# Two products of a decoder block, from packed float32 parts to scaled float16 parts

## The chip, the cores and the metric

One core of a Trainium2 chip runs the whole block as one program. The metric is the device time of one execution in microseconds (us); three timed executions are given, and one further execution was recorded by the profiler. Engines are named as the profile does: PE is TensorE (PEld its weight loads), DVE is VectorE, ACT is ScalarE, POOL is GpSimd, and SP is SyncE, which issues most transfers.

## The reference, cut to what matters

The block normalises its input, multiplies it by one wide matrix, runs dilated attention and a causal convolution side by side, merges the two under sigmoid gates, mixes the result, and ends with a SwiGLU layer. All is float32 with 1024 tokens and 1024 channels. The part around the change is:

```python
o = einsum('gbsh,gbshd->bshd', alpha, stack(outs))        # attention output, 1024 x 512
y_attn = o @ w_attn_out                                   # 512 x 1024: the attention output's product
y_conv = silu(layer_norm(conv(u))) @ w_conv_out + b_conv_out
merged = sigmoid(z_ga) * y_attn + sigmoid(z_gc) * y_conv
x = x + rms_norm(merged @ w_mix_out, g_post_mix)          # 1024 x 1024: the mixing product
h = rms_norm(x, g_pre_ffn)
x = x + rms_norm((silu(gate) * up) @ w_ffn_out, g_post_ffn)   # gate, up from h @ w_ffn_in
```

## The kernel before, in words

Every product is made of two-part operands: a value is split into a rounded first part (hi) and the remainder (lo), and a product is hi by hi, hi by lo and lo by hi, three matmuls. Most products have float16 parts, scaled by powers of two from sums of squares so that nothing leaves float16's range: `two` gives one buffer for both parts, `scaled_parts` writes hi on ACT (L330) and lo on DVE (L331). The attention output's product (jobs `ao`), the mixing product (jobs `mx`) and the last product of the block have packed float32 parts without a scale instead: hi by a copy on ACT (L320), lo by a subtraction (L321) on DVE for a weight tile's first half and on the engine `wsplit` for its second, which is POOL in these two products.

The order of the work on each engine is that of the Python program. `tick` is called after every three matmuls; it advances generators that stand in the background (`bg`), such as `early_scales`, `merge` and `mix_norm`, each of which yields the number of ticks until its next step. So the program's text sets where in each engine's queue a step stands, and the times set only who waits.

The stages, with start and end in us of the profiled span:

- 206 to 331, gate pairs (`gate_pair`): two-by-two products by Winograd's scheme (`winograd`, matmuls at L501 to L503), whose bank X is filled, copied by ACT (L515, L520, L525) and filled again, while DVE runs the convolution (L885) and POOL prepares sums.
- 331 to 540, query and key pairs, in the same scheme. `early_scales` runs behind them: it loads 20 weight tiles of 128x1024 (12 of the value weights, 8 of the convolution's output weights) one after another, ACT squares and sums each (L208), and at the end of a group DVE makes the scale.
- 540 to 853, value products, attention (exponentials L1251, transposes L1274, evictions L1279), and the convolution's output product (L485 to L489, as all products by `unit`). For each of four pairs of heads `merge` adds the three dilations' outputs into O[0], a tile of 128x1024, PE transposes it (L1363) and ACT evicts it (L1366). The first two go to DRAM and come back through `out_parts`, the last two are split at once.
- 853 to 897, the attention output's product: eight column blocks n, two halves of 512 tokens each, 12 matmuls per half. DVE multiplies each half by the attention's gate (L1753) and adds the convolution's half under its gate (L1754); ACT makes hi of the sum (L1756), DVE lo (L1759), one half later. There are six PSUM banks of the kind that products use.
- 897 to 990, the mixing product (L1794): row tiles 0 and 1 together, while the weight tiles arrive, then six tiles one by one, 48 matmuls each. After each tile `mix_norm` runs in the background: `residual` (Square on ACT at L1492, `rstd_rows` at L1479 to L1484, DVE at L1499 and L1503), then Square and scaling of the new row (L1514, L1516), and after four tiles transposes (L1524) with eviction on ACT (L1530).
- 990 to 1617, the SwiGLU layer, which the diff doesn't touch.

`total` and `bound` turn partial sums of the 128 partitions into one power of two: PE multiplies a column by a matrix of ones (L146), DVE halves the exponent (L147, L149).

The lines have other numbers in the changed kernel. Those of which the text speaks: L208 becomes L230; L320, L321 and L330, L331 become L381 and L382; L515, L520, L525 become L566, L571, L576; L1251 becomes L1302; L1279 becomes L1330; L1366 becomes L1424; L1753, L1754, L1756, L1759 become L1814, L1815, L1817, L1820; L1492 becomes L1552. The Square in `merge` is L1406.

Of the kernel before, what the change touches and what calls it, by code (L numbers as in the profile page):

```python
# [9 lines left out]
F32 = mybir.dt.float32  # L10
# [8 lines left out]
T = 1024  # L19
# [52 lines left out]
class Build:  # L72
# [77 lines left out]

    def scales(self, i):
# [15 lines left out]
    def input_scales(self):  # L167
# [4 lines left out]
        for c in (C_PRE, C_PREF):  # L172
            m = self.tiny(2, "pk", 4)
            nc.scalar.activation(self.junk[:, :8], self.col8(c), AF.Square, scale=1 / H_TOP, accum_out=m[:, 0:1])
            p.append(self.total(m, 1))
        yield 6
        for e, c in enumerate((C_PRE, C_PREF)):
# [3 lines left out]
            self.bound(t[:, 0:1], p[e])  # L181
# [9 lines left out]
    def early_scales(self, groups):  # L191

        nc = self.nc
        m = self.small.tile([128, 24], F32, name="em")
        t = self.small.tile([128, 5], F32, name="cs")
        self.conv_bias = self.small.tile([128, 8], F32, name="cb")
        for c, x, k in ((0, C_GLN, 32), (1, C_BLN, 1)):
            nc.scalar.activation(self.junk[:, :8], self.col8(x), AF.Square, scale=k * A_TOP, accum_out=m[:, c:c + 1])
        pa = self.total(m[:, 0:2], 2)
        yield 6  # L200
        self.bound(t[:, 0:1], pa)
        nc.vector.reciprocal(t[:, 1:2], t[:, 0:1])
        yield 2
        todo = [(e, j) for e, jobs in enumerate(groups) for j in jobs]
        x, ends = None, {len(jobs) + 2 + sum(len(y) for y in groups[:e]): e for e, jobs in enumerate(groups)}
        for n in range(2, len(todo) + 3):
            if x is not None:
                nc.scalar.activation(self.junk, x, AF.Square, scale=W_TOP, accum_out=m[:, n - 1:n])  # L208
            x = None
            if n < len(todo) + 2:  # L210
                x = self.slot()
                nc.sync.dma_start(x, self.jobs[todo[n - 2][1]][0])
            yield 3
            if n in ends:
# [10 lines left out]
                for j in jobs:  # L225
                    self.scale[j] = tuple(u[:, i:i + 1] for i in range(1, 5))
            else:
                yield 8
        w = self.scale[groups[1][0]][0]
        nc.vector.tensor_tensor(t[:, 4:5], t[:, 0:1], u[:, 0:1], op=OP.mult)  # L230
        nc.vector.tensor_scalar(self.conv_bias, self.col8(C_BCO), t[:, 1:2], w, op0=OP.mult, op1=OP.mult)
        nc.vector.tensor_scalar(self.vun, self.scale[groups[0][0]][1], 1 / (KEEP * P_TOP), None, op0=OP.mult)
        self.act_scale, self.conv_un = t[:, 1:2], t[:, 4:5]
# [1085 lines left out]
    def merge(self, hp, st, last):  # L1319
# [34 lines left out]
        yield 2 + 2 * late  # L1354
        if hp < 2:
            hi = self.slot()
        else:
            hi, lo = self.slot(F32R), self.slot(F32R)
# [826 lines left out]
```

## Time and profile before

| | us |
|---|---|
| median of three timed executions | 1623.63 (1623.48 to 1623.65) |
| the profiled execution, its own time | 1622.73 |
| its span, first to last instruction | 1621.0 |
| PE, DVE, ACT, POOL busy | 1594.3, 1244.2, 997.3, 448.8 |
| mean granted clock of TensorE | 0.998 |

The profiled execution lies 0.9 us below the median, and its span 1.7 us below its own time. Busy time of PE is that of pipelined matmuls whose recorded durations overlap: how fast they follow one another is read from start to start. In a row of a timeline a bracket gives the idle time of the engine ahead of the instruction and who ended it; in the chain a row has start, duration, engine and line, and a count where rows were joined.

### The profile page before, as it was taken

What the parts mean: (1) busy time and instruction counts of PE and PEld (TensorE: products, weight loads), DVE (VectorE), ACT (ScalarE), POOL (GpSimd) and SP (SyncE); (2) the same over time, 40 slices, a digit from 0 to 9 for tenths busy, and PEclk for the clock granted to TensorE, in tenths of its full rate; (3) what the DMA queues carried; (4) which work ended last, traced back from release to release, by engine and by line L of the source; (5) the groups of instructions that cost most, each with busy time, mean ns of one, the idle gap of its engine ahead of it and who ended that gap; (6) DMA issues with size and microseconds to landing.
All of it is one profiled execution on the core that took longest, in us unless ns stands there. A gap on an engine that the chain in (4) does not pass through costs nothing.

```text
span 1621.0 us, 25348 instructions
## 1 busy us (share of the span) xinstructions
PE 1594.3 (98%) x9034; PEld 980.5 (60%) x9034; DVE 1244.2 (77%) x2415; ACT 997.3 (62%) x1900; POOL 448.8 (28%) x372
## 2 busy tenths in 40 slices
PE   8999999999999999999999999999999999999998
PEld 6744444444444799976658786444444444588886
DVE  6879999988898768797777655876666666667686
ACT  6476666777776578877743576645455555444453
POOL 0006777767777343654401200000000000000000
PEclk9999999999999999999999999999999999999999
DMA  4352333455665666768847422043222331684334
GB/s 175 109 208 104 111 136 144 151 188 188 202 181 144 215 189 171 179 209 242 256 153 269 180 95 91 27 146 127 104 98 98 130 124 72 233 305 118 136 105 156
DMA packets 158906, 254.02 MB, mean 157 GB/s; under 512 B 63313, under 2 KB 82444, under 8 KB 158780
## 3 DMA queue, kind: packets, MB, share of 16 engines
q1 hardware_dynamic: 154572, 240.23, 44.5%
q0 software_dynamic: 3920, 11.91, 2.3%
q8 instruction: 71, 1.16, 0.3%
q14 instruction: 55, 0.45, 0.1%
q10 hardware_dynamic: 288, 0.27, 0.0%
HBM read 178.52 MB, written 78.55 MB: 159 GB/s over the span
## 4 chain that ended last, share of the span: by engine, by line
PE 83%; DVE 8%; ACT 3%; POOL 2%; issue 2%; DMA 1%; SPq 0%; DVEq 0%; POOLq 0%; ACTq 0%
PE p L2069 13%; PE p L501 13%; PE p L503 13%; PE p L502 13%; PE p L1794 4%; PE p L485 4%; PE p L489 4%; PE p L487 4%; PE p L1142 2%; PE p L1144 2%; PE p L1146 2%; DVE p L885 2%; PE p L739 2%; PE p L1274 2%; PE p L1237 2%
## 5 line engine op out<-in xcount | busy, mean ns | idle before, releaser
L501 PE MATMUL p<-b,b 128*128 128x512 f16 x1032 | 390.9, 379 | 2.1 <-ACT c L515 1.6
L503 PE MATMUL p<-b,b 128*128 128x512 f16 x1032 | 391.1, 379 | 1.5 <-POOL b L340 1.5
L502 PE MATMUL p<-b,b 128*128 128x512 f16 x1032 | 391.0, 379 | 0.0
L2069 PE MATMUL p<-b,b 128*128 128x512 f32 x924 | 211.4, 391 | 1.9 <-DVE c L1977 1.9
L2069 PEld LDWEIGHTS p<-b,b 128*128 128x128 f32 x924 | 174.5, 189 | 38.8 <-DVE c L1977 2.3
L503 PEld LDWEIGHTS <-b 128*128 128x128 f16 x1032 | 100.8, 98 | 125.3 <-POOL b L340 4.0
L501 PEld LDWEIGHTS <-b 128*128 128x128 f16 x1032 | 100.9, 98 | 121.3
L502 PEld LDWEIGHTS <-b 128*128 128x128 f16 x1032 | 100.8, 98 | 119.2 <-issue 3.0
L885 DVE SCALAR_TENSOR_TENSOR p<-b,par,p 128x511 f32<-128x511 f32 (+14 forms) x232 | 164.5, 742 | 0.0
L485 PE MATMUL p<-b,b 128*128 128x512 f16 (+1 forms) x368 | 141.3, 384 | 1.6 <-ACT b L330 1.6
L489 PE MATMUL p<-b,b 128*128 128x512 f16 (+1 forms) x368 | 140.7, 382 | 0.4 <-DVE b L331 0.4
L487 PE MATMUL p<-b,b 128*128 128x512 f16 (+1 forms) x368 | 140.6, 382 | 0.0
L331 DVE SCALAR_TENSOR_TENSOR b<-d,sc,b 128x1024 f16<-128x1024 f32 x40 | 51.2, 1281 | 87.7 <-ACT b L330 87.7
L340 POOL TENSOR_TENSOR b<-d,b 128x1024 f16<-128x1024 f32 x44 | 93.9, 2133 | 83.8 <-ACT b L339 83.8
L1146 PE MATMUL p<-b,b 128*128 128x256 f16 x384 | 104.7, 273 | 0.0
L1142 PE MATMUL p<-b,b 128*128 128x256 f16 x384 | 104.7, 273 | 0.0
L1144 PE MATMUL p<-b,b 128*128 128x256 f16 x384 | 104.7, 273 | 0.0
L1399 ACT CAST b<-b 128x512 fp32r<-128x512 f32 (+1 forms) x117 | 72.1, 617 | 43.4 <-PE p L2069 20.4
L1400 DVE TENSOR_TENSOR b<-b,b 128x512 fp32r<-128x512 f32 (+1 forms) x117 | 80.1, 688 | 19.6 <-ACT b L1399 18.2
L1794 PE MATMUL p<-b,b 128*128 128x512 f32 x384 | 90.2, 392 | 0.0
L1251 ACT ACTIVATE c<-c,stat 128x128 f32<-128x128 f32 (+1 forms) x192 | 84.3, 443 | 6.8 <-DVE stat L1241 6.7
L515 ACT COPY c<-p 128x512 f32<-128x512 f32 x43 | 25.2, 585 | 99.6 <-PE p L503 64.1
(296 smaller groups left out, 3431.9 us busy)
## 6 DMA issues: line engine op xcount, KB each, us to landing
b<-w_in SPq DMA_DIRECT2D x30, 512.0 KB, 5.7
b<-w_v SPq DMA_DIRECT2D x24, 512.0 KB, 4.6
b<-w_fi SPq DMA_DIRECT2D x24, 512.0 KB, 4.4
d<-w_in SPq DMA_DIRECT2D x23, 512.0 KB, 3.6
dqS<-c SPq DMA_DIRECT2D x44, 256.0 KB, 2.0
b<-w_fo SPq DMA_DIRECT2D x44, 256.0 KB, 4.9
c<-dqS SPq DMA_DIRECT2D x44, 256.0 KB, 4.4
d<-w_fi SPq DMA_DIRECT2D x20, 512.0 KB, 3.7
```

The source lines that it names most:

```text
L485: nc.tensor.matmul(ps, hi[:, s], a, start=kt == 0, stop=False)
L487: nc.tensor.matmul(ps, hi[:, s], b, start=False, stop=False)
L489: nc.tensor.matmul(ps, lo[:, s], a, start=False, stop=kt == nk - 1)
L501: nc.tensor.matmul(ps, hi[:, s], a, start=first and kt == 0, stop=False, skip_group_check=True)
L502: nc.tensor.matmul(ps, hi[:, s], b, start=False, stop=False, skip_group_check=True)
L503: nc.tensor.matmul(ps, lo[:, s], a, start=False, stop=kt == 3, skip_group_check=True)
L885: nc.vector.scalar_tensor_tensor(A[i][:, j:], src[i][:, :H - j], w[i], A[i][:, j:], op0=OP.mult, op1=OP.add)
L1142: nc.tensor.matmul(o, a, hi[:, s], start=kt == 0, stop=False)
L1144: nc.tensor.matmul(o, a, lo[:, s], start=False, stop=False)
L1146: nc.tensor.matmul(o, b, hi[:, s], start=False, stop=kt == KT - 1)
L1794: nc.tensor.matmul(banks[tt][nh], st, wt[:, nh * H:(nh + 1) * H], start=bool(kt == 0 and a), stop=bool(kt == KT - 1 and b))
L2069: nc.tensor.matmul(acc[t], x, y, start=first and e == 0, stop=last and e == 2, skip_group_check=True)
```

## The change

Both products take two float16 parts under powers of two. Their matmuls keep their number and shapes, 192 and 384.

- The jobs `ao` and `mx` join the set of float16 jobs, so their weights are split by `scaled_parts`, ACT and DVE, each half; POOL has no part in it any more (15 subtractions fewer). Each product's operands lie in one buffer where there were two.
- `early_scales` has four groups (12, 8, 8, 8 tiles), 36 loads and Squares for 20, starts with the gate pairs and has one tile every 12 ticks for 13. It also makes constant factors for what follows.
- In each `merge` ACT squares O[0] with a running sum ahead of the transposes' evictions; the evictions apply a scale. After the last merge `mix_scales` (one transpose on PE, nine operations on DVE) makes the mixing product's scale from the four sums.
- In the attention output's product L1753 and L1759 become operations with a scale, L1756 a scaled copy.
- `residual` has one more DVE multiply of 128x1 (rr by the factor that takes the scale out), and its Square's scale comes from a tile.
- `root` and `largest` take the place of `total` and `bound` in `input_scales` and `early_scales`: a 128x128 transpose on PE and a maximum on DVE for the matmul with ones.

```diff
     def early_scales(self, groups):
...
-        for n in range(2, len(todo) + 3):
+        for n in range(len(todo) + 1):
             if x is not None:
-                nc.scalar.activation(self.junk, x, AF.Square, scale=W_TOP, accum_out=m[:, n - 1:n])
+                k = self.jobs[todo[n - 1][1]][1]
+                nc.scalar.activation(self.junk[:, :k], x[:, :k], AF.Square, scale=W_TOP, accum_out=m[:, n - 1:n])
...
-                yield 8
+                yield 7
...
+    def mix_scales(self):
+        nc = self.nc
+        r, on = self.osq[:, 4:5], self.osq[:, 5:6]
+        nc.vector.tensor_reduce(r, self.osq[:, :4], AX.X, OP.add)
+        yield 4
+        self.root(on, r)
+        y = self.mix_un
+        nc.vector.scalar_tensor_tensor(y, on, self.att_top, self.conv_top, op0=OP.mult, op1=OP.add)
+        self.power(y, y)
+        nc.vector.tensor_scalar(y, y, 2.0 ** -14, TINY, op0=OP.mult, op1=OP.max)
+        nc.vector.reciprocal(self.mix_scale, y)
+        nc.vector.tensor_tensor(y, y, self.mix_w, op=OP.mult)
+        nc.vector.tensor_scalar(self.mix_root, y, ROOT, None, op0=OP.mult)
...
         yield 2 + 2 * late
+        nc.scalar.activation(self.junk, O[0], AF.Square, scale=self.o_scale, accum_out=self.osq[:, hp:hp + 1])
...
-            hi, lo = self.slot(F32R), self.slot(F32R)
+            hi, lo = self.two(T)
...
-            nc.scalar.copy(a, y)
             if hp > 1:
-                nc.vector.tensor_tensor(lo.rearrange("p (m u) -> p u m", u=8)[:, h * 4:h * 4 + 4], y, f(a),
-                                        op=OP.subtract)
+                nc.scalar.activation(a, y, AF.Copy, scale=self.o_scale)
+                nc.vector.scalar_tensor_tensor(lo.rearrange("p (m u) -> p u m", u=8)[:, h * 4:h * 4 + 4], y,
+                                               self.o_scale, a, op0=OP.mult, op1=OP.subtract)
+            else:
+                nc.scalar.copy(a, y)
...
-            self.OT[hp] = self.both(x)
+            self.OT[hp] = self.both(x, self.o_scale, True)
...
         r = self.rstd_rows(ss[:, 1:2], ss[:, 2:3])
+        nc.vector.tensor_tensor(r, r, self.mix_un, op=OP.mult)
...
-    B.f16 = {*range(glu_jobs[3][0], ao[0]), *range(B.fi0, len(J))}
-    B.early = [i for p in vj.values() for i in p] + co
+    B.f16 = {*range(glu_jobs[3][0], len(J))}
+    B.early = [i for p in vj.values() for i in p] + co + ao + mx
...
+    es = B.bg(B.early_scales((B.early[:12], co, ao, mx)))
     for n in range(4):
         B.gate_pair(B.d_ga[2 * n:2 * n + 2], ga[n])
...
-            nc.vector.tensor_tensor(c[:, s], ps, c[:, s], op=OP.mult)
+            nc.vector.scalar_tensor_tensor(c[:, s], ps, B.att_un, c[:, s], op0=OP.mult, op1=OP.mult)
             nc.vector.scalar_tensor_tensor(c[:, s], y[:, s], B.conv_un, c[:, s], op0=OP.mult, op1=OP.add)
-            x = B.slot(F32R)
-            nc.scalar.copy(x[:, :H], c[:, s])
+            x = B.packed()
+            nc.scalar.activation(x[:, :H], c[:, s], AF.Copy, scale=B.mix_scale)
...
-            rest = lambda x=x, c=c[:, s]: nc.vector.tensor_tensor(x[:, H:], c, f(x[:, :H]), op=OP.subtract)
+            rest = lambda x=x, c=c[:, s]: nc.vector.scalar_tensor_tensor(x[:, H:], c, B.mix_scale, x[:, :H],
+                                                                         op0=OP.mult, op1=OP.subtract)
```

Where the instructions stand now is shown at three places; a row has line, operation, output and input with buffer numbers, and the tile's shape (x2: two such in a row).

ACT in a gate pair, before and after, from the scaling of a gate half to the second copy of bank X. The tile em collects the weights' sums.

```order
L339 CAST b_1987<-d_1953 128x1024
L978 ACTIVATE c_1843<-c_1843,sc_1693 128x512
L995 ACTIVATE c_2001<-p_1840,sc_1693 128x512
L515 COPY c_2005<-p_2003 128x512
L165 ACTIVATE d_1922<-d_1922,sc_2019 128x1024
```

```order
L390 CAST b_2016<-d_1982 128x1024
L1029 ACTIVATE c_1845<-c_1845,sc_1695 128x512
L1046 ACTIVATE c_2030<-p_1842,sc_1695 128x512
L230 ACTIVATE junk,em<-b_1974 128x1024
L566 COPY c_2034<-p_2032 128x512
L187 ACTIVATE d_1949<-d_1949,sc_2048 128x1024
```

A weight Square (L230) stands ahead of the copy of bank X; another stands ahead of the next pair's copies at other points, since 12 ticks don't divide a pair.

ACT in the first merge (hp = 0), before and after: exponentials (L1251, now L1302), evictions of transposed exponentials (L1279, now L1330), and the eviction of the merged output's transposes (L1366, now L1424).

```order
L1279 ACTIVATE c_8299<-p_8294 128x512
L330 ACTIVATE b_8259<-b_8003,es_4900 128x512
L1366 COPY b_8315<-p_8316 128x4x128
L1251 ACTIVATE c_8276,stat_7727<-c_8276,stat_7727 128x256 x2
L1279 ACTIVATE c_8344<-p_8339 128x512
```

```order
L1330 ACTIVATE c_8391<-p_8386 128x512
L381 ACTIVATE b_8351<-b_8095,es_3588 128x512
L1406 ACTIVATE junk,osq<-b_8048,cs 128x1024
L1424 COPY b_8408<-p_8409 128x4x128
L1302 ACTIVATE c_8368,stat_7819<-c_8368,stat_7819 128x256 x2
L1330 ACTIVATE c_8437<-p_8432 128x512
```

The Square of O[0] (L1406) stands ahead of the eviction, and so ahead of the exponentials behind it.

DVE at the last column block (n = 7) of the attention output's product and behind it, before and after; es is the scale of the mixing weights.

```order
L321 TENSOR_TENSOR b_10634<-b_10579,b_10633 128x512
L1753 TENSOR_TENSOR b_10581<-p_10629,b_10581 128x512
L1754 SCALAR_TENSOR_TENSOR b_10581<-b_10583,cs,b_10581 128x512
L1759 TENSOR_TENSOR b_10624<-b_10527,b_10624 128x512
L1753 TENSOR_TENSOR b_10581<-p_10653,b_10581 128x512
L1754 SCALAR_TENSOR_TENSOR b_10581<-b_10583,cs,b_10581 128x512
L1759 TENSOR_TENSOR b_10650<-b_10581,b_10650 128x512
L1759 TENSOR_TENSOR b_10668<-b_10581,b_10668 128x512
L321 TENSOR_TENSOR b_10703<-b_10627,b_10702 128x512
L321 TENSOR_TENSOR b_10723<-b_10672,b_10722 128x512
```

```order
L382 SCALAR_TENSOR_TENSOR b_10721<-b_10669,es_4890,b_10721 128x512 x2
L1814 SCALAR_TENSOR_TENSOR b_10671<-p_10717,cs,b_10671 128x512
L1815 SCALAR_TENSOR_TENSOR b_10671<-b_10673,cs,b_10671 128x512
L1820 SCALAR_TENSOR_TENSOR b_10695<-b_10620,cs,b_10695 128x512
L1814 SCALAR_TENSOR_TENSOR b_10671<-p_10740,cs,b_10671 128x512
L1815 SCALAR_TENSOR_TENSOR b_10671<-b_10673,cs,b_10671 128x512
L1820 SCALAR_TENSOR_TENSOR b_10737<-b_10671,cs,b_10737 128x512 x2
L382 SCALAR_TENSOR_TENSOR b_10788<-b_10715,es_4890,b_10788 128x512 x2
L382 SCALAR_TENSOR_TENSOR b_10807<-b_10758,es_4890,b_10807 128x512 x2
```

Each weight tile takes two operations of DVE where one was DVE's and one POOL's.

More of the change, by code (lines that the diff above doesn't have):

```diff
@@ L172, in input_scales @@
         for c in (C_PRE, C_PREF):
-            m = self.tiny(2, "pk", 4)
-            nc.scalar.activation(self.junk[:, :8], self.col8(c), AF.Square, scale=1 / H_TOP, accum_out=m[:, 0:1])
-            p.append(self.total(m, 1))
+            p.append(self.largest(1 / H_TOP, c))
         yield 6
@@ L1373, in merge @@
             self.OT[hp] = hi, lo
+            if hp == 3:
+                assert self.measured == 4
+                yield from self.mix_scales()
         else:
             self.nc.gpsimd.dma_start(self.d_ot[hp], hi)
+    measured = 0
     def out_parts(self):
@@ L1491, in residual @@
         for nh in range(2):
-            nc.scalar.activation(out[:, nh * H:(nh + 1) * H], banks[nh], AF.Square, scale=ROOT, accum_out=ss[:, nh:nh + 1])
+            nc.scalar.activation(out[:, nh * H:(nh + 1) * H], banks[nh], AF.Square, scale=self.mix_root, accum_out=ss[:, nh:nh + 1])
         yield gap
@@ L1665, in build @@
     B.CONV = (1, 1, 1, 0, 1)
-    es = B.bg(B.early_scales((B.early[:12], co)))
     for g in range(3):
```

66 lines of the change are left out of this document (50 added, 16 removed).

## The prediction

> **What bounds the kernel now.** I read the engines' shares and the chain that ended last first, then the table by stage, then the steps of TensorE from row to row, and last the waits in each place that the diff touches.
>
> ```profile
> PE 1594.3 (98%) x9034; PEld 980.5 (60%) x9034; DVE 1244.2 (77%) x2415; ACT 997.3 (62%) x1900; POOL 448.8 (28%) x372
> ...
> PE 83%; DVE 8%; ACT 3%; POOL 2%; issue 2%; DMA 1%; SPq 0%; DVEq 0%; POOLq 0%; ACTq 0%
> ```
>
> TensorE (PE) is busy for 98% of the span and carries 83% of the chain, so a shorter matmul is worth its difference wherever TensorE is kept fed, and work on VectorE (DVE) or ScalarE (ACT) costs only where it makes TensorE wait. The stages that the diff touches (us of the stretch; busy us per engine in the order PE, PEld, DVE, ACT, POOL):
>
> ```profile
> 206.00:331.00 125.00, 125.00 (x588) 56.75 (x587) 117.53 (x199) 87.69 (x136) 94.98 (x61) 1.00 0.42 152
> ...
> 540.00:715.00 175.00, 174.46 (x1943) 158.40 (x1942) 139.34 (x363) 134.99 (x359) 86.73 (x102) 1.00 0.68 200
> ...
> 853.00:897.00 44.00, 44.00 (x196) 36.40 (x195) 34.58 (x53) 14.46 (x30) 7.16 (x8) 1.00 0.77 272
> 897.00:918.00 21.00, 21.00 (x95) 17.38 (x94) 11.51 (x13) 13.44 (x29) 9.24 (x6) 1.00 0.55 214
> 918.00:990.00 72.00, 70.23 (x327) 57.12 (x325) 43.29 (x136) 42.93 (x86) 0.00 (x0) 1.00 0.26 89
> ```
>
> These are the gate pairs, V products with attention, the attention output's product, the mixing product's first two row tiles, and its other six. TensorE has no gap in the first, third and fourth, and the clock column stands at 1.00 in all, so a step of one stage compares with a step of another.
>
> **The step of a matmul.** Rows of TensorE (start, duration), then of the chain (start, duration, count):
>
> ```profile
> 853.32 0.40 PE L487 MATMUL p<-b,b 128*128 128x512 f32 x1
> ...
> 1202.94 0.38 PE L501 MATMUL p<-b,b 128*128 128x512 f16 x1
> ...
> 1211.79 0.38 PE L503 MATMUL p<-b,b 128*128 128x512 f16 x1
> ```
>
> ```profile
> 896.82 21.55 PE p L1794 x95
> ...
> 966.09 0.66 PE p L1524 x4
> 966.75 1.39 PE p L1794 x6
> 968.14 0.44 PE p L1524 x4
> 968.58 21.80 PE p L1794 x96
> ```
>
> Float16 at 512 columns: 41 steps from 1202.94 to 1211.79, 215.9 ns each. Packed float32: 21.55/95 = 226.8 ns in the mixing product, and 191 steps from 853.32 to 896.82 in the attention output's product, 227.7 ns. The durations (0.38 to 0.40) overlap and aren't the pace.
>
> Here I weigh a page. The Trainium skill, "TensorE: Matmul & The Clock Gate", Back-to-back issue gap, gives 215.7 ns for an isolated warm matmul of 512 columns, and about 131 ns for a sustained stream that loads weights between; the trace agrees with the first and shows nothing near the second. By the second, 576 matmuls would save 55 us, estimated as 576 x (227 - 131).
>
> **The sum, term by term.**
>
> 1. Attention output's product, 192 matmuls: 191 x (227.7 - 215.9) = -2.25 us. TensorE had no gap, six banks stand between it and VectorE, so a VectorE that is late does not stop it here. Bounds: -2.25 and 0.
>
> 2. Mixing product, tiles 0 and 1: 95 x (226.8 - 215.9) = -1.04 us before waits (term 4).
>
> 3. The other 288 matmuls could save 288 x 10.9 = 3.1 us. But ScalarE and VectorE work through one tile's norm after another in series:
>
> ```profile
> 935.85 0.58 ACT L1492 ACTIVATE d<-p 128x512 f32<-128x512 f32 x1
> ...
> 944.40 0.58 ACT L1492 ACTIVATE d<-p 128x512 f32<-128x512 f32 x1
> ...
> 951.88 1.15 ACT L1516 ACTIVATE b<-d,rr 128x1024 f32<-128x1024 f32 x1 [0.87 <-DVE rr L1484]
> 952.94 0.58 ACT L1492 ACTIVATE d<-p 128x512 f32<-128x512 f32 x1
> ```
>
> ```profile
> 953.89 0.60 PE L1524 MATMUL p<-ident,b 128*128 128x128 f32 x4
> ...
> 966.09 0.66 PE L1524 MATMUL p<-ident,b 128*128 128x128 f32 x4 [1.05 <-ACT b L1530]
> ```
>
> Each L1492 starts the moment the tile before is through (8.55 us a tile), so until 953 these two are behind and set the pace. The fourth tile's L1516 ends at 953.03, and TensorE's first transpose that reads it starts at 953.89: it can come 0.86 us earlier, no more. Against that stands the new multiply in every residual, one 128x1 operation of some 0.16 us by the row of L1480 below, in the series of four tiles: 0.6 us. So 0.2 us is left there. From there to 966 the evictions on ScalarE hold TensorE (1.05 us waited): nothing. After 966.09, 6 + 96 matmuls run with TensorE first again: 102 x 10.9 = -1.1 us. Taken: -1.3 us; bounds -3.1 (the series isn't in the way) and +0.6 (only the multiplies count).
>
> ```profile
> 933.63 0.16 DVE L1480 TENSOR_TENSOR rr<-ss,eps_rms 128x1 f32<-128x1 f32 x1 [2.26 <-ACT b L1514]
> ```
>
> 4. The second halves of the weights leave GpSimd (POOL) for VectorE. VectorE's rows of before, near the end of the attention output's product:
>
> ```profile
> 884.41 0.68 DVE L1753 TENSOR_TENSOR b<-p,b 128x512 f32<-128x512 f32 x1
> 885.12 0.75 DVE L1754 SCALAR_TENSOR_TENSOR b<-b,cs,b 128x512 f32<-128x512 f32 x1
> 885.79 0.69 DVE L1759 TENSOR_TENSOR b<-b,b 128x512 fp32r<-128x512 f32 x1
> 886.40 0.68 DVE L1753 TENSOR_TENSOR b<-p,b 128x512 f32<-128x512 f32 x1
> ...
> 894.79 0.69 DVE L321 TENSOR_TENSOR b<-b,b 128x512 fp32r<-128x512 f32 x1 [0.60 <-ACT b L320]
> ...
> 897.78 0.68 DVE L1753 TENSOR_TENSOR b<-p,b 128x512 f32<-128x512 f32 x1
> 898.49 0.75 DVE L1754 SCALAR_TENSOR_TENSOR b<-b,cs,b 128x512 f32<-128x512 f32 x1
> 899.16 1.52 DVE L1759 TENSOR_TENSOR b<-b,b 128x512 fp32r<-128x512 f32 x2
> 900.60 0.68 DVE L321 TENSOR_TENSOR b<-b,b 128x512 fp32r<-128x512 f32 x1
> ```
>
> ```profile
> 872.18 0.43 DVE L321 TENSOR_TENSOR b<-b,b 128x256 fp32r<-128x256 f32 x1 [0.45 <-ACT b L320]
> ```
>
> A unit is 1.99 us of VectorE (884.41 to 886.40). L1753 and L1759 become the scalar form that L1754 shows (0.75 for 0.69): about 2.12 us. A column block n is two units, 4.24 us, plus two parts of 256 columns, 0.76 (0.43 from the row and the scalar form's 0.06 more, overlapped as the rows are), plus the 0.45 for ScalarE's first half, which stays: 5.45 us. TensorE needs 24 x 0.2159 = 5.18. So VectorE loses 0.27 us per block, 2.2 over eight; block 4 has four such parts (+0.76), and blocks 5 and 6 two of 512 columns (0.67 each, +0.6 a block): together some 4.1 us, less what idle time at the start takes up, say 3.2 more than now. Now the last eviction starts 1.0 us after the mixing product begins (897.78 against 896.82), then 4.2 us after. Behind it stand L1815, two remainders and the two parts of the third weight tile: 0.78 + 0.67 + 1.35 + 1.35, so that tile is ready at 8.35 us, while TensorE wants it after 26 steps, 5.6 us. TensorE waits: +2.7 us, of which I take 2.5, since ScalarE's side may run ahead a little. Before, that tile came at 901.3 from VectorE and no gap followed. Bounds: 0 (VectorE keeps up, as the 9.4 idle us in the third row of the stage table allow on the face of it) and +4.
>
> 5. A Square over 128x1024 stands in each merge ahead of the transposes' evictions. Its price is that of the weight squares of before; the second fence shows TensorE's waits at the first merge.
>
> ```profile
> 375.63 1.04 ACT L208 ACTIVATE junk<-b 128x1024 bf16<-128x1024 f32 x1
> 376.57 0.19 ACT L208 ACTIVATION_READ_ACCUMULATOR junk<-b 128x1 f32 x1
> ```
>
> ```profile
> 717.13 0.66 PE L1363 MATMUL p<-ident,b 128*128 128x128 f32 x4 [0.91 <-DVE c L1287]
> ...
> 719.20 0.65 PE L1274 MATMUL p<-ident,c 128*128 128x128 f32 x4 [0.55 <-DVE c L1287]
> ```
>
> 1.16 us of ScalarE each. Two merges lie in attention, where TensorE already waits; behind the Square queue the exponentials (L1251) and evictions (L1279) of the next heads, whose readers are VectorE and then TensorE. I take 0.45 each, between 0 (the heads in flight cover it) and 1.2: +0.9, bounds 0 and +2.4. The other two merges, and the scale after the last one, lie in the convolution's output product beside slack: 0; without it, one Square, 1.2.
>
> 6. The weight squares grow from 20 to 36 and begin with the gate pairs: one load and one Square per 12 ticks there, some 16. ScalarE's waits in 206 to 331:
>
> ```profile
> ACT c L515 <- PE p L503: 10.3, 7, 1.8
> ACT c L525 <- PE p L503: 9.0, 7, 1.5
> ACT b L339 <- POOL d L360: 8.8, 6, 1.7
> ACT c L520 <- PE p L503: 5.2, 7, 1.1
> ```
>
> 16 x 1.16 = 18.6 us go into 37 idle us; the order puts them ahead of copies for which ScalarE waits 1.3 to 1.5 us in the mean (10.3/7, 9.0/7), so most fit. Queues passed: SyncE issues 16 loads of 512 KB more (8 of 256 KB and 8 of 512 KB in all) into a stage with DMA at 0.42. Taken +0.3; bounds -0.6 (qk pairs relieved a little) and the slower rival's.
>
> 7. Small edits, at nothing: the two 128x128 transposes in place of one-column matmuls, the tiny scale operations, ScalarE's scaled copy for a cast (same engine, same size). Attention's and the norm's slack hides them; without it some 25 x 0.16 = 4 us of VectorE in a stage with 7.5 idle.
>
> Sum: -2.25 - 1.04 - 1.3 + 2.5 + 0.9 + 0.3 = -0.9. The profiled execution took 1622.73 us (span 1621.0), so 1621.8; the median of the runs is 0.9 above it: **1622.7 us**.
>
> **Rivals.**
> - Faster: VectorE keeps pace in term 4, and heads in flight cover term 5. Then 1622.7 - 2.5 - 0.9 = 1619.3; with the whole of term 3, 1617.5. For it: no gap in 853 to 918 now. Against: the reckoned 5.45 against 5.18. Chance 0.31.
> - Slower: Squares in the gate pairs delay a bank's copy. X is written again one product (12 steps, 2.59 us) after the product that filled it, and the copy takes 0.59; so a queue of more than 2.0 us ahead of that copy (L515 and L525, in the changed kernel L566 and L576) stops TensorE: a Square plus one other full-width operation. If 5 of 16 fall so, at 1.16 each: +5.8, 1628.5. The waits above speak against, VectorE's 94% (117.5 of 125) for it. Chance 0.13. The same page of the Trainium skill, Architectural detail, has ScalarE and VectorE as strict queues, first in, first out; ScalarE's rows here stand in the program's order, so the trace agrees.
> - The step stays at 226.8 (the loads of weights, now instructions of their own, or late parts set it): 1622.7 + 4.6 = 1627.3. Chance 0.03; other float16 products of this kernel all run at 215.9.
> - The 131 ns of the Trainium skill's sustained stream, about 1570 us by the estimate above: no chance, since 41 steps of this kernel's own stream, with a weight load before each, are at 215.9.
>
> **How the numbers follow.** The forecast has 0.53, with a range of its own of 1620.4 to 1625.4 (terms 4 to 6 at their ends, one at a time). About 0.2% (3.2 us, so below 1620.4 or above 1626.9) can be told from no change. Faster 0.31 (the first rival), slower 0.16 (second and third), same 0.53. The range that leaves out 2 in 10 cuts the faster rival below 1618.6 and the slower one above 1626.8.
>
> **What would show it.** Right: steps of 215.9 ns in both products, a wait of TensorE near the third weight tile with L382 as releaser, VectorE's last L1814 3 to 5 us into the mixing product, added waits of about half a us near the first two merges, none in the gate pairs. Wrong: no wait at the start of the mixing product (faster), or waits of L501 on L566 or L576 in the gate pairs (slower).

## The result, and the profile after

The changed kernel is slower: 1633.88 us median (1631.82 to 1636.27, six runs) against 1623.37 (1620.86 to 1623.65, six runs), a ratio of 1.0071 with a 95% interval of 1.0059 to 1.0082. No change was forecast, at 1622.7 us with a range to 1626.8: it was wrong, by 11 us. The profiled execution took 1631.82 us, the shortest of the six, so about 2 us of the median are not in its trace; the other five have no trace, but the experiments' traces show two pieces of about that size (below). The experiments were timed in three groups (1 to 4, 5 to 8, 9 to 11), each beside the kernel before, whose medians were 1622.80, 1622.47 and 1622.74: differences between groups are good to about 1 us.

The page of the changed kernel, then its table by stage (columns as before: us of the stretch, busy us of PE, PEld, DVE, ACT, POOL, clock, DMA share and rate):

```profile
span 1629.8 us, 25433 instructions
...
PE 1590.1 (98%) x9038; PEld 929.5 (57%) x9038; DVE 1264.0 (78%) x2475; ACT 1025.4 (63%) x1936; POOL 432.7 (27%) x357
```

```profile
206.00:331.00 125.00, 123.60 (x580) 56.11 (x580) 118.02 (x202) 102.01 (x161) 94.08 (x60) 1.00 0.58 211
331.00:540.00 209.00, 206.80 (x972) 93.78 (x971) 186.00 (x342) 152.85 (x256) 149.41 (x95) 1.00 0.58 167
715.00:853.00 138.00, 131.64 (x1173) 84.13 (x1172) 108.17 (x303) 99.69 (x287) 42.22 (x56) 1.00 0.61 194
```

TensorE is busy for 4.2 us less and the span is 8.8 us longer: there are 13 us more in which it does nothing. Both programs issue the same 6172 matmuls of 512 columns in the same order, so the start of each can be compared with the start of the same one before. The difference at the end of a stage, less that at its start, says where the time went (us, profiled executions, minus is faster):

| stage (in the kernel before) | forecast | changed kernel | evictions token by token | the same, and early_scales later | the same, and remainders one unit later | the last version |
|---|---|---|---|---|---|---|
| start, to 190 | 0 | +0.82 | +0.40 | +0.99 | +0.49 | +0.81 |
| to 331, gate pairs | +0.3 | +1.67 | +3.58 | +0.18 | +0.21 | +0.18 |
| to 540, query and key pairs | 0 | +1.37 | +3.00 | -0.34 | -0.37 | -0.31 |
| to 830, values, attention | +0.9 | +1.51 | +1.29 | +1.27 | +1.28 | +1.27 |
| to 853, convolution's output product | 0 | +5.19 | +0.11 | +0.11 | +0.11 | +0.11 |
| to 897, attention output's product | -2.25 | -2.13 | -2.13 | -2.13 | -2.13 | -2.13 |
| to 918, mixing product, tiles 0, 1 | +1.46 | +3.25 | +4.48 | +4.79 | -0.37 | -1.04 |
| to 990, the other six tiles | -1.3 | +0.21 | +0.19 | -0.10 | +1.55 | -0.70 |
| to 1395, feed-forward layer | 0 | +0.65 | +0.64 | +0.64 | -0.01 | +0.64 |
| to the end, last product | 0 | -3.68 | -3.68 | -3.66 | -3.66 | -3.65 |
| sum | -0.9 | +8.87 | +7.87 | +1.74 | -2.90 | -4.83 |

The last five columns are the changed kernel and experiments 1, 7, 9 and 11. The first row is scatter: a kernel that differs from the one before in its last product alone (experiment 4) shows +0.64 there. The +0.6 in the feed-forward layer was not followed up.

**The largest piece, 5.2 us**, is in a step that the prediction put at nothing: the evictions of the late merges' transposes. Groups of instructions of the changed kernel in 825 to 862 (count, busy us, mean ns), then the same step before in 825 to 856:

```profile
L1420 ACT ACTIVATE b<-p,cs 128x512 f16<-128x512 f32 x4 | 10.1, 2537 | 0.6 <-issue 0.6
L1421 DVE SCALAR_TENSOR_TENSOR b<-p,cs,b 128x512 f16<-128x512 f32 x4 | 10.0, 2506 | 3.7 <-ACT b L1420 3.7
```

```profile
L1368 DVE TENSOR_TENSOR b<-p,b 128x512 fp32r<-128x512 f32 x4 | 4.4, 1097 | 1.7 <-ACT b L1366 1.7
L1366 ACT CAST b<-p 128x512 fp32r<-128x512 f32 x4 | 4.4, 1091 | 7.5 <-issue 4.7 <-PE p L1363 2.7
```

2.5 us instead of 1.1, eight times. The chains behind them are late, and TensorE's waits in 835 to 865 (total, times, longest) show it; in the same step before there was none. The profile names no releaser for the first (issue); that it hangs on the evictions is shown by experiment 1.

```profile
PE p L1416 <- issue: 2.4, 1, 2.4
PE p L155 <- DVE osq L275: 1.7, 1, 1.7
PE p L536 <- DVE b L1788: 0.4, 1, 0.4
```

**The start of the mixing product** has the wait that was forecast, but larger. TensorE, VectorE and ScalarE of the changed kernel:

```profile
905.09 3.45 PE L1856 MATMUL p<-b,b 128*128 128x512 f16 x15
908.78 2.10 PE L1856 MATMUL p<-b,b 128*128 128x512 f16 x9 [0.24 <-DVE b L382]
913.71 0.38 PE L1856 MATMUL p<-b,b 128*128 128x512 f16 x1 [2.82 <-ACT b L381]
```

```profile
888.66 0.88 DVE L382 SCALAR_TENSOR_TENSOR b<-b,es,b 128x256 f16<-128x256 f32 x2 [0.53 <-ACT b L381]
...
894.29 1.68 DVE L382 SCALAR_TENSOR_TENSOR b<-b,es,b 128x256 f16<-128x256 f32 x4 [0.53 <-ACT b L381]
...
900.94 1.42 DVE L382 SCALAR_TENSOR_TENSOR b<-b,es,b 128x512 f16<-128x512 f32 x2 [0.74 <-ACT b L381]
...
907.31 1.42 DVE L382 SCALAR_TENSOR_TENSOR b<-b,es,b 128x512 f16<-128x512 f32 x2 [0.74 <-ACT b L381]
...
910.76 0.74 DVE L1814 SCALAR_TENSOR_TENSOR b<-p,cs,b 128x512 f32<-128x512 f32 x1
```

```profile
912.32 0.72 ACT L1817 ACTIVATE b<-b,cs 128x512 f16<-128x512 f32 x1 [1.39 <-DVE b L1815]
912.95 1.32 ACT L381 ACTIVATE b<-b,es 128x512 f16<-128x512 f32 x2
```

After 24 matmuls TensorE stops for the third weight tile's first part, which ScalarE can begin only behind the last operand (L1817), which waits for VectorE. VectorE takes 5.6 us for a block with two parts of 256 columns (888.66 to 894.29), 6.4 for one with 512 (900.94 to 907.31), TensorE needs 5.18 (24 steps of 215.9 ns); the last eviction starts 5.7 us after the mixing product.

**Attention** lost most of its 1.51 us at the first merge, where TensorE waits for an eviction that stands behind the Square:

```profile
727.15 0.66 PE L1325 MATMUL p<-ident,c 128*128 128x128 f32 x4 [0.70 <-ACT b L1424]
```

From start to start this is 0.92 us; at the second merge 0.2 to 0.3 are lost.

**The gate pairs and the query and key pairs** each have one wait of TensorE for a bank that VectorE reads late. TensorE's two rows, then VectorE ahead of the second:

```profile
207.40 0.38 PE L552 MATMUL p<-b,c 128*128 128x512 f16 x1 [1.44 <-DVE c L1036]
...
500.51 0.38 PE L552 MATMUL p<-b,c 128*128 128x512 f16 x1 [2.04 <-DVE p L1100]
```

```profile
495.07 0.16 DVE L246 RECIPROCAL es<-es 128x1 f32<-128x1 f32 x1
495.15 1.93 DVE L247 TENSOR_SCALAR es<-hs,es 128x3 f32<-128x3 f32 x1
```

The second row is a 128x3 operation that took 1.93 us; the shortest of its kind take 0.21, in the kernel before too, where some (L158) took up to 1.75. With the other small operations behind it, the last step of early_scales takes 4.4 us of VectorE between 494.69 and 499.76, ahead of L1100. VectorE is busy for 118.0 of 125 us in the first of these stages and 186.0 of 209 in the second. Ahead of the first wait stand two such runs, of 128x1 operations and of reading a 128x128 transpose, at 198.89 and 202.84, 1.4 us together.

### The profile page after: what moved, and what is told of

Same layout as the page of the kernel before. It is cut to its first block, busy times and chain, and to the rows that moved or that the text cites. A ratio compares the mean times of both kernels' runs of the same rounds, so it can differ in the third digit from the quotient of the medians.

```text
span 1629.8 us, 25433 instructions
## 1 busy us (share of the span) xinstructions
PE 1590.1 (98%) x9038; PEld 929.5 (57%) x9038; DVE 1264.0 (78%) x2475; ACT 1025.4 (63%) x1936; POOL 432.7 (27%) x357
## 5 line engine op out<-in xcount | busy, mean ns | idle before, releaser
L552 PE MATMUL p<-b,b 128*128 128x512 f16 x1032 | 390.9, 379 | 1.6 <-ACT c L566 1.6
L554 PE MATMUL p<-b,b 128*128 128x512 f16 x1032 | 391.1, 379 | 1.4 <-POOL b L391 1.4
L553 PE MATMUL p<-b,b 128*128 128x512 f16 x1032 | 391.0, 379 | 0.0
L2131 PE MATMUL p<-b,b 128*128 128x512 f32 x924 | 209.9, 389 | 0.0
L382 DVE SCALAR_TENSOR_TENSOR b<-d,sc,b 128x1024 f16<-128x1024 f32 x40 | 51.2, 1281 | 87.8 <-ACT b L381 87.8
L1856 PE MATMUL p<-b,b 128*128 128x512 f16 x384 | 86.9, 384 | 3.6 <-ACT b L381 3.1
L1302 ACT ACTIVATE c<-c,stat 128x128 f32<-128x128 f32 (+1 forms) x192 | 84.4, 444 | 6.4 <-DVE stat L1292 6.3
L566 ACT COPY c<-p 128x512 f32<-128x512 f32 x43 | 25.2, 585 | 93.3 <-PE p L554 59.2
```

The source lines that it names most:

```text
L552: nc.tensor.matmul(ps, hi[:, s], a, start=first and kt == 0, stop=False, skip_group_check=True)
L553: nc.tensor.matmul(ps, hi[:, s], b, start=False, stop=False, skip_group_check=True)
L554: nc.tensor.matmul(ps, lo[:, s], a, start=False, stop=kt == 3, skip_group_check=True)
L1856: nc.tensor.matmul(banks[tt][nh], st, wt[:, nh * H:(nh + 1) * H], start=bool(kt == 0 and a), stop=bool(kt == KT - 1 and b))
L2131: nc.tensor.matmul(acc[t], x, y, start=first and e == 0, stop=last and e == 2, skip_group_check=True)
```

## The experiments

**1. Evictions token by token.** Same values, same places, another order of writing: four float16 values side by side, then the next token, instead of one value every 16 bytes.

```diff
+                y = ps.rearrange("p (u m) -> p m u", u=4)
+                a = hi.rearrange("p (m u) -> p m u", u=8)[:, :, h * 4:h * 4 + 4]
                 nc.scalar.activation(a, y, AF.Copy, scale=self.o_scale)
```

> The changed kernel, but the two late merges' evictions walk the tile token by token, so that four float16 values in a row are written beside each other instead of one every 16 bytes; the values are the same. Theory: the float16 evictions take 2.5 us instead of 1.1 because each 2-byte value goes to a place of its own, 16 bytes from the next. Then L1420 and L1421 fall to 1.2 us or less, TensorE's 2.6 us wait for the last merge's transposes goes, and the execution gets 2.5 to 4 us shorter than the changed kernel's. Rival: the operand with the scale, or the conversion on the way out of PSUM, costs it. Then they stay at 2.5 us and the time stays within 0.5 us.

```profile
L1423 DVE SCALAR_TENSOR_TENSOR b<-p,cs,b 128x512 f16<-128x512 f32 x4 | 3.0, 746 | 2.2 <-ACT b L1422 2.2
L1422 ACT ACTIVATE b<-p,cs 128x512 f16<-128x512 f32 x4 | 2.7, 687 | 2.3 <-PE p L1416 1.8 <-issue 0.6
```

1629.74 us (1.0043, 1.0026 to 1.0060), 4.1 less. The evictions took 0.69 and 0.75 us, with the scale and the conversion as they were, less than the float32 ones before, and no wait is left in 835 to 865. The rival is out: the scattered 2-byte write was the cost. Whether the smaller value or the closer spacing (16 bytes for 32) makes it worse than the float32 write was not tried apart.

This trace has a second wait of TensorE in the gate pairs, 1.75 us at 317.85 for L1036, which the changed kernel's profiled execution lacks. The two kernels don't differ there; the traces do, in one small operation of VectorE and what ran on POOL. Changed kernel, then here:

```profile
307.45 0.21 DVE L247 TENSOR_SCALAR es<-hs,es 128x3 f32<-128x3 f32 x1
308.30 2.14 POOL L391 TENSOR_TENSOR b<-b,b 128x1024 f16<-128x1024 f32 x1 [2.96 <-ACT b L390]
```

```profile
308.14 1.90 DVE L247 TENSOR_SCALAR es<-hs,es 128x3 f32<-128x3 f32 x1
307.88 2.13 POOL L391 TENSOR_TENSOR b<-b,b 128x1024 f16<-128x1024 f32 x1 [3.02 <-ACT b L390]
```

Here POOL's operation began 0.26 us ahead of L247 and L247 ended with it; VectorE reaches L1036 2.4 us later (317.11 for 314.73).

**2. Written in the transposes' order, read with a stride.**

```diff
-            a = hi.rearrange("p (m u) -> p u m", u=8)[:, h * 4:h * 4 + 4]
+            a = hi[:, h * 512:h * 512 + 512]
...
+  x.rearrange("p (u m) -> p m u", u=8)[:, hf * 64:hf * 64 + 64]   # the matmul's moving operand, kt 2 and 3
```

> The changed kernel, but the two late merges write their float16 tiles in the transposes' own order, 512 values in a row, and the matmuls that read these tiles as their moving operand walk them with a stride of 128 values. Theory of the strided write: L1420 and L1421 fall to 0.6 to 0.75 us, the gain is that of the first experiment or a little more (3 to 4.5 us), unless the strided read slows the matmuls, in which case the 96 matmuls on these tiles show steps above 216 ns. Rival (scale operand or conversion): they stay near 2.5 us.

1708.76 us (1.0529, 1.0513 to 1.0545). The evictions took the same 0.69 and 0.75 us as in the first, but the matmuls on the strided tiles step by 0.86 us instead of 0.216, at a granted clock of 1.00 (864 to 868):

```profile
865.56 1.04 PE L536 MATMUL p<-b,b 128*128 128x512 f16 x1
866.42 1.04 PE L538 MATMUL p<-b,b 128*128 128x512 f16 x1
```

96 such steps are 62 us of the 80 that the stage lost against experiment 1; most of the rest is unstrided matmuls between them at 0.43 us a step (869.04 to 870.32), where the granted clock was 0.50. So here the order has to be put right on the way out of PSUM, not on the way into TensorE.

**3. No Squares in the merges.**

```diff
-        nc.scalar.activation(self.junk, O[0], AF.Square, scale=self.o_scale, accum_out=self.osq[:, hp:hp + 1])
...
-                yield from self.mix_scales()
...
+        yield from self.mix_scales()      # at the end of early_scales, from constant sums
```

> The changed kernel without the four Squares of the merged attention output (L1406); their sums are a constant, and the mixing scale is worked out with the other scales during the query and key pairs, not after the last merge. The numbers of the scale are thus not measured. Theory: the merges' Squares cost 1.2 us of TensorE's time in attention (the wait at the first merge), and the scale behind the last merge costs the 1.7 us wait of its transpose, since it stands in VectorE's queue behind two slow evictions: 3 us less in all, with the 2.4 us wait for the last merge's transposes left. Rival: all that was lost at the merges is the slow evictions' doing. Then this gains under 1 us.

1636.26 us (1.0084, 1.0069 to 1.0099): slower than the changed kernel, where 3 us less was expected. By stages the theory holds: attention loses 0.13 us instead of 1.51, and of the waits in the convolution's output product the 1.7 us one is gone and the 2.4 us one left (+2.9 for +5.2). What gave it back is not in the merges: the last product's -3.68 became -0.01, the gate pairs showed the second wait (L247 at 307.54 took 1.88 us), and the query and key pairs and the start of the mixing product lost 1.9 and 1.7 us more than in the changed kernel's trace, much as in experiment 1. The first of these needed an experiment of its own.

**4. The kernel before, its last product's banks named in the other order.**

```diff
     B.banks(y=4, x=4)
-    B.bank("y")
```

> The kernel before with one line less: the last product's PSUM banks are named without the unused allocation ahead of them, which swaps the two sets of four physical banks, so that its first matmul goes to a bank that has been free for some time instead of the one that L1977 reads last. Theory: the 2.2 us wait at 1400 us and the eight matmuls at half the pace behind it (1.5 us) in the kernel before, both absent from the changed kernel, hang on that bank alone. Then this kernel is 3.7 us faster than before, 1619.7 against 1623.4. Rival: TensorE waits there for the operands of the last product, so nothing changes.

1619.06 us against 1622.80 (0.9981, 0.9971 to 0.9990): 3.7 us faster with nothing but a change of banks. TensorE's first rows of the last product, before and here:

```profile
1402.66 5.54 PE L2069 MATMUL p<-b,b 128*128 128x512 f32 x16 [1.85 <-DVE c L1977]
```

```profile
1401.04 5.16 PE L2068 MATMUL p<-b,b 128*128 128x512 f32 x21
```

Before, the first matmul takes the bank that L1977 reads last: a wait of 1.85 us, and then 16 matmuls in 5.54 us (granted clock 0.55 in 1403 to 1406.8) where 21 fit into 5.16. The two programs show why the changed kernel is spared: before, and in experiment 3, the last half of the convolution's output product already lies in the set of banks that the program names once the merges are over; in the changed kernel the merges take more steps, the set is named behind that half, every later bank is another, and the wait is gone by chance (the last product starts with the same bank in all three; only in the changed kernel is it not the one used last). The gain of 3.7 us in the changed kernel thus has nothing to do with float16.

**5. The end of early_scales spread over 20 ticks** (on the first experiment's kernel).

```diff
+        yield 4
         nc.vector.tensor_tensor(t[:, 3:4], t[:, 0:1], cu, op=OP.mult)
...
+        yield 4        # likewise in three more places of the run
```

> The kernel of the first experiment (evictions token by token), with the tiny VectorE operations at the end of early_scales spread over 20 ticks instead of 2. Theory: that run of some fifteen operations, three of which take 1.2 to 1.9 us beside POOL instead of 0.2, holds VectorE for 5 us at 495 us, so that L1100 reads its bank late and TensorE waits 2.0 us and then runs eight matmuls at half the pace. Spread, the wait goes: 2.0 to 3.6 us less than the first experiment's kernel. Rival: the bank that TensorE takes next (the order of the banks) makes the wait, not the operations. Then it stays, or another comes.

1627.27 us (1.0028, 1.0017 to 1.0040), 2.5 less; the stage went from +3.00 to -0.50 and no wait is left at 500. In the first experiment that wait was followed by matmuls at half the pace (TensorE's rows there), which is 1.4 of the 3.5 us:

```profile
502.00 0.38 PE L552 MATMUL p<-b,c 128*128 128x512 f16 x1 [2.03 <-DVE p L1100]
...
503.15 0.63 PE L553 MATMUL p<-b,c 128*128 128x512 f16 x1
503.57 0.63 PE L554 MATMUL p<-b,c 128*128 128x512 f16 x1
```

**6. Second remainders back on POOL** (on the first).

```diff
+                nc.scalar.activation(hi[:, s], r[:, s], AF.Copy, scale=self.scale[i][0])
+                nc.scalar.activation(r[:, s], r[:, s], AF.Copy, scale=self.scale[i][0])
+                nc.gpsimd.tensor_tensor(lo[:, s], r[:, s], hi[:, s], op=OP.subtract)
```

> The kernel of the first experiment, with the remainders of the weight tiles' second halves back on POOL in the two products: ACT makes the first part, then scales the raw half in place, and POOL subtracts. Theory: VectorE is 4 us late at the end of the attention output's product because it has these remainders too, and ScalarE's first part of the third weight tile stands behind its last operand. With 0.37 to 0.67 us less per tile VectorE is at most 1.5 us late, and TensorE's waits at the start of the mixing product (3.4 us and 1.3 us of half pace) go: 3 to 4.5 us less. Rival: ScalarE is the late one there (its wait is the one that the profile names). Then a further ScalarE operation per tile makes it worse or leaves it.

1633.94 us (1.0073, 1.0056 to 1.0090), 4.2 more. My theory fell here: relieving VectorE did not help, the start of the mixing product lost 6.93 us instead of 4.48, with POOL and ScalarE as releasers (TensorE's waits, 895 to 930):

```profile
PE p L1863 <- POOL b L372: 3.1, 3, 1.4
PE p L1863 <- ACT b L386: 1.9, 1, 1.9
```

The rival named ScalarE, and the added ScalarE operation is part of that loss, so this alone doesn't acquit VectorE.

**7. early_scales with the query and key pairs again** (on the first): started where it was before, one tile every 8 ticks, all 36 Squares there.

```diff
-    es = B.bg(B.early_scales((B.early[:12], co, ao, mx)))      # ahead of the gate pairs
+    es = B.bg(B.early_scales((B.early[:12], co, ao, mx)))      # ahead of the query and key pairs
...
-                yield 7
+                yield 3
```

> The kernel of the first experiment, with early_scales started before the query and key pairs, as in the kernel before, and one tile every 8 ticks instead of 12 so that all 36 are done in time. Theory: the waits in the gate pairs (1.4 us at 205 us and, in this kernel, 1.8 us at 316 us) come from early_scales' work there, VectorE being 94% busy. Then they go, 3 us less to about 570 of the query and key pairs, where 36 Squares in 209 us may cost up to 3 us anew. Rival: they are the whole of the Squares' cost wherever these stand. Then the query and key pairs lose as much as the gate pairs win.

1623.26 us (1.0007, 0.9998 to 1.0016), 6.5 less, the largest step of all. Of the two stages' +6.58 in the first experiment -0.16 is left. TensorE's waits in 200 to 545, there and here:

```profile
PE p L552 <- DVE c L1036: 3.2, 2, 1.8
PE p L552 <- DVE p L1100: 2.0, 1, 2.0
```

```profile
PE p L1193 <- ACT p L1106: 0.7, 1, 0.7
```

So 36 Squares in 209 us cost nothing there, and the rival is out. All of early_scales moved here, so the experiment doesn't part the Squares from the scales' small VectorE steps. The traces do in part: each of the waits that went had VectorE as its releaser, with such steps ahead of it. One L247 still took 1.55 us (at 445.59), without a wait of TensorE behind it, so where these steps fall decides. Whether the Squares, by holding ScalarE, set when POOL's operations meet them stays open.

**8. Experiments 5 and 6 together.**

> The fifth and the sixth experiment's edits together. If the two causes are apart, their gains add: 5 to 8 us less than the first experiment's kernel, 1622 to 1625 us. If one wait merely moves to the other place, it is no better than the better of the two.

1631.12 us (1.0053, 1.0038 to 1.0068). From the first experiment's 1629.74, -2.5 and +4.2 give 1631.4: the two places are apart and their effects add. The 5 to 8 us less did not come, since one of the two is a loss.

**9. Remainders one unit later** (on the seventh): the order in VectorE's queue alone.

```diff
+                for c in range(2):
+                    self.pieces.append((j, lambda j=j, c=c: self.part_hi(j, c)))    # ACT
+                for c in range(2):
+                    self.pieces.append((j, lambda: None))
+                for c in range(2):
+                    self.pieces.append((j, lambda j=j, c=c: self.part_lo(j, c)))    # DVE
```

> The seventh experiment's kernel (evictions token by token, early_scales with the query and key pairs), with each weight tile's two remainders on VectorE one unit of the attention output's product later than its two first parts on ScalarE; nothing is added or taken away. Theory: in each block VectorE waits 0.5 to 0.7 us for a first part that ScalarE can't begin before its last operand, which itself waits for VectorE; these waits, eight of them, and not VectorE's work, make it 4 us late. Without them it is 1 to 2 us late, and the waits at the start of the mixing product (3.6 us and 1.3 us at half pace) shrink by 2 to 5 us: 1618.5 to 1621.5. Rival: VectorE's work alone fills the blocks. Then the lateness falls by less than 1 us and the time stays at 1623.

1619.14 us (0.9982, 0.9972 to 0.9991), 4.1 less. The first two tiles went from +4.79 to -0.37, and TensorE now starts the mixing product with 27 matmuls in a row; the last eviction (L1842 here) starts 2.1 us behind it instead of 5.7:

```profile
896.25 6.22 PE L1884 MATMUL p<-b,b 128*128 128x512 f16 x27
902.75 2.53 PE L1884 MATMUL p<-b,b 128*128 128x512 f16 x11 [0.29 <-DVE b L400]
```

```profile
898.30 0.75 DVE L1842 SCALAR_TENSOR_TENSOR b<-p,cs,b 128x512 f32<-128x512 f32 x1
```

In experiment 7 too the eviction was 5.7 us late. Nothing but the order changed here, so the lateness was mostly VectorE waiting for ScalarE, which waited for VectorE. Part of the gain is also that TensorE's matmuls there no longer ran at half pace, as six did behind the wait in experiments 1 and 7.

**10. A weight tile more ahead of the last unit** (on the ninth): `B.ahead = int(n >= 4) + int(n >= 7)` for `int(n >= 5)`.

> The ninth experiment's kernel with one weight tile more of the mixing product made ahead of the last unit, so that the third tile's parts stand in front of the last operands in the queues of ScalarE and VectorE. Theory: the wait at the start of the mixing product hangs on the third tile standing behind the last operands; then no wait is left there, 0 to 2 us less than the ninth. Rival: the wait moves to the fourth tile or to the last operands, since VectorE has the same work. Then it is within 0.5 us of the ninth.

1619.26 us (0.9983, 0.9974 to 0.9993), no different from the ninth: the rival's case in time, though not for its reason. The wait did go (108 matmuls in a row), and the six tiles behind lost half of what the first two won (-1.04 and +1.90 for -0.37 and +1.55); the rest is within the scatter.

**11. The feed-forward scales a little later** (on the tenth): `35 + 4 * e` for `35 + 3 * e`.

> The tenth experiment's kernel with the scales of the feed-forward layer's first four weight tiles one to three ticks later each (35 + 4e ticks for 35 + 3e). Theory: in the mixing product TensorE waits 2.1 us with a one-column matmul (L146) for a small bank that VectorE reads behind the first tiles' norms, and the eight matmuls behind it run at half the pace; with the fourth of them 3 ticks later (1.9 us) the wait shrinks to about 0.5 us and the half pace goes: 2 to 3 us less than the tenth. Rival: the norms' chain on ScalarE and VectorE sets the time there, so the wait moves to the first transposes of the new rows and the time stays.

1618.29 us (0.9977, 0.9967 to 0.9986), about 1 less than the tenth where 2 to 3 were expected. TensorE's row of the fourth scale, in the tenth and here:

```profile
927.80 0.16 PE L146 MATMUL p<-pb,ones 128*128 128x1 bf16 x1 [2.11 <-DVE sc L147]
```

```profile
928.63 0.16 PE L146 MATMUL p<-pb,ones 128*128 128x1 bf16 x1 [0.73 <-DVE sc L147]
```

The wait shrank as expected, and 0.5 us of it came back at the first transposes of the new rows (1.4 us waited for 1.0), a little of the rival. But no matmul ran at half pace behind L146 in the tenth's trace, so that part of the theory was wrong there. Its half pace lies behind a later wait for the transposes, 2.6 us in both; TensorE's next matmuls, in the tenth and here:

```profile
967.24 2.06 PE L1884 MATMUL p<-b,b 128*128 128x512 f16 x6
```

```profile
965.94 1.46 PE L1884 MATMUL p<-b,b 128*128 128x512 f16 x6
```

The granted clock in 968 to 971.5 was 0.52 in the tenth and 1.00 here. The six tiles gain 2.6 us from trace to trace: 1.4 by the shorter wait, less the 0.5, and 1.7 by this half pace, which one execution had and the other had not behind the same wait. The medians differ by 1.0, so the half pace is not a gain of the edit as far as these runs show.

## Why the prediction was wrong

- **Term 7 failed, and it is the largest.** "ScalarE's scaled copy for a cast (same engine, same size)" was put at nothing, and the place where it differs was in front of me: the write's pattern. At 2 bytes every 16 the eight evictions cost 1.4 us more each, together 5.1 us of TensorE's time (experiment 1 gives them back). The scale after the last merge (ten operations of VectorE), put at nothing in term 5, waited in VectorE's queue behind them, 1.7 us of the 5.2.
- **Term 1 held**: -2.13 us for -2.25. The step of 215.9 ns came as read.
- **Terms 2 and 4 had the right place and VectorE's lateness, mis-sized, and the wrong last link**: +3.25 for +1.46. The wait's releaser was to be VectorE's L382; 3.1 of the 3.6 us waited for ScalarE's L381, above all the third tile's first part behind the last operand. A block took 5.6 and 6.4 us for my 5.45 and about 6; I counted ScalarE's wait as 0.45 throughout, and it is 0.53 for first parts of 256 columns and 0.74 for 512. The last eviction came 5.7 us into the mixing product for 4.2. Half-paced matmuls behind the wait weren't in the sum either: the profiled execution has none there, experiment 1 has six (+4.48).
- **Term 3**: of the 3.1 us nothing came (+0.21, forecast -1.3). The wait at L146 grew from 0.7 to 2.1 us and pulled half-paced matmuls behind it; with the wait at 0.7 again and no half pace in its trace, experiment 11 gets -0.70.
- **Term 5 held roughly, within its bounds**: +1.29 to +1.51 for +0.9, and experiment 3 (+0.13) shows that it is the Squares. It is not 0.45 at each merge but about 0.9 at the first and 0.2 to 0.3 at the second.
- **Term 6 had the right place, the wrong cause.** The slower rival named Squares ahead of the copies of bank X. No wait on L566 or L576 came in the gate pairs; what stopped TensorE there were banks that VectorE read late, behind small operations of early_scales that term 7 had put at nothing: 1.4 us in the profiled execution and 1.7 to 1.8 us more, at 316, in the traces of experiments 1, 2, 3, 5, 6 and 8. The query and key pairs, at 0 in the forecast, lost 1.4 us in the same way.
- **Not in the sum at all: -3.68 us** from banks given out in another order, a gain of chance that hid almost a third of the loss.

In the trace the forecast is out by 9.8 us (8.87 against -0.9): 5.2 at the evictions, 1.8 and 1.5 in the mixing product's two parts, 1.4 each in the gate pairs and in the query and key pairs, 2.2 in smaller stages and the scatter of the first, less the 3.7 of the banks.

What float16 is worth here when its waits are removed: experiment 11 has 1618.29 against 1622.74 before, but 3.7 us of the 4.4 are the banks', which experiment 4 gets without float16 (1619.06). The two were not run side by side and lie 0.8 us apart; whether the change itself gains anything stays open.

## What to carry to other kernels

When an operand gets narrower, look at how it is written and read, not only at its shape: a permuting eviction that is passable in 4 bytes can more than double in 2, and is cured by putting the contiguous index innermost. Where two engines hand work to each other in turn, look for the wait before the work: here moving the dependent half one step back in the queue took it away, with as much work as before. And compare the start of every matmul with the same one before: gains and losses of chance, such as a bank that happens to be free, stand out there and not in the total.

## What the runs showed of the hardware

- 128x512 out of PSUM into a permuted tile: 1.09 us as 4-byte values every 32 bytes, 2.5 us as 2-byte values every 16 bytes, 0.69 us (ACT) and 0.75 us (DVE) in runs of four 2-byte values, though PSUM is then read with a stride, and the same when both sides are contiguous (experiment 2).
- A float16 moving operand with a stride of 256 bytes: 0.86 us a step instead of 0.216 at a granted clock of 1.00; over the stretch the clock then fell to 0.74 and 0.68 in the mean (860 to 900 and 900 to 980).
- Waits of 1.85 to 2.8 us were followed by four to eight steps of 0.43 us in some places (behind 2.03 us at 502 in experiment 1, granted clock 0.50 in 502.7 to 505.8) and not in others (2.04 us at 500 in the changed kernel, clock 1.00). The Trainium skill, "TensorE: Matmul & The Clock Gate", What's actually happening, tells of a free-running window of 3.4 us that decides; a wait shorter than that window being enough here, and only sometimes, is what these traces show, and it may be a part of why the kernel before scatters from 1620.6 to 1623.7.
- Small VectorE operations (TENSOR_SCALAR) of 128x3 and 128x8 took 0.1 to 0.4 us where no two-input operation of POOL ran and up to 1.9 us where one did. In the thirteen traces 199 of them took over 0.5 us, and each ended 0.02 to 0.03 us behind the end of a two-input operation of POOL that was running when it began (experiment 1: POOL from 307.88 to 310.01, L247 from 308.14 to 310.04). Those of 128x1 beside POOL, in the gate and the query and key pairs, stayed at or below 0.22 us. No experiment took POOL's operation away.
